# Grouped-query attention on one core: K transposed by the DMA engines instead of TensorE, with a new order of TensorE's work

## The chip, the cores and the metric

The kernel runs on one core of a Trainium2 chip. Times are device microseconds of one execution. A core has TensorE (PE, matmuls; PEld is its weight load), VectorE (DVE), ScalarE (ACT), GpSimd (POOL), SyncE (SP, which here only issues DMAs) and 16 DMA engines. Every "fast" run below is compared with fast runs of the kernel before on the same chip.

## The reference

Batch 8, sequence 512, 32 query heads, 8 KV heads, head dimension 64, all fp32. Four query heads share one KV head.

```python
scores  = einsum('bhqd,bhkd->bhqk', Q, K_expanded) / sqrt(64)
weights = exp(scores - max(scores))
weights = weights / (sum(weights) + 1e-10)
output  = einsum('bhqk,bhkd->bhqd', weights, V_expanded)
```

## The kernel before

Work is cut into 32 units (a batch and a pair of KV heads). A unit has 16 *score tiles* (128 keys x 2 heads x 512 queries). For each tile PE writes scores into one of three buffers in PSUM, the memory that its results go to. Then ACT (11 tiles of a unit) or DVE (5 tiles, with integer arithmetic that approximates the exponential) turns them into probabilities in SBUF, the core's working memory, and so frees the buffer. A unit also has 32 *output blocks*, each of four matmuls of probabilities with V, which fill one of two small output banks that DVE copies out.

Q and K come from HBM with the sequence on the partitions. Before they can be used in a score matmul they must be turned, so that the head dimension is on the partitions. PE does that with transposing matmuls (*turns*) into the same two output banks, and DVE copies the result out: 16 turns of Q and 4 of K per unit.

```python
def load_k(b):
    t = kn_pool.tile([128, SC, KV * D], BF16, name="k_nat")
    nc.gpsimd.dma_start(out=t, in_=rows(K, b, 0, KV))     # fp32 -> bf16, natural layout
    kn[b] = t
...
def mm_turn(f, at):                                       # one PE transpose, into an output bank
    ...
    nc.tensor.transpose(xs[f][:, at * 128:(at + 1) * 128], src, ident)

def take_turn(f):
    ...
    if part is None:                                      # K: DVE copy, then a swapped copy by DMA
        k = kt_pool.tile([128, 2, S], BF16, name="kt")
        nc.vector.tensor_copy(out=k[:, 0, :], in_=x[:, 0:S])
        nc.sync.dma_start(out=k[64:128, 1, :], in_=k[0:64, 0, :])
        nc.sync.dma_start(out=k[0:64, 1, :], in_=k[64:128, 0, :])
```

The program gives every engine its instructions in a fixed order. A small planner in Python sets that order when the kernel is built. Its inputs are lists per unit: `SCORES` says which of 16 tiles goes to ACT (A) or DVE (D), `FILL` how many output blocks or turns PE does behind each tile, `ORDER` the order of those (`o7` is seven output blocks that share a bank, `K4` four turns of K, `08` and `18` eight turns of Q).

```python
SCORES = "ADAAADAADAADAADA"
FILL = [0, 0, 8, 0, 0, 6, 9, 0, 0, 8, 0, 0, 12, 0, 0, 9]
ORDER = "K4 o6 o7 08 o7 18 o5 o7".split()
```

The softmax here doesn't subtract the row's maximum and nothing guards it: scores larger than these inputs give would overflow.

## Time and profile before

| | |
|---|---|
| time | 351.09 us, median of 3 (later 350.81, median of 12) |
| ACT, first to last exponential | 7.95 to 341.99 us of a span of 349.3 |
| ACT's period per unit, units 2 to 29 | 10.35 us |

The page of the kernel before: busy time of each engine, then the chain of work that ended last (by engine), then ACT's group of exponentials (busy us, mean ns of one; idle time before them and its releaser).

```profile
PE 337.0 (96%) x5774; PEld 224.6 (64%) x5774; DVE 329.3 (94%) x463; ACT 333.9 (96%) x356; POOL 280.3 (80%) x201
...
PE 48%; ACT 38%; POOL 4%; DVE 4%; issue 3%; DMA 1%; POOLq 0%; DVEq 0%; ACTq 0%
...
L288 ACT ACTIVATE pa<-s 128x1024 bf16<-128x1024 f32 x353 | 331.4, 1026 | 4.1 <-PE s L275 3.5
```

Four engines are busy for 80 to 96% of the span, so busy shares do not name the bottleneck. And ACT's idle time of 4.1 us is not all that it loses: the records (mean 1026 ns) overlap, so a small wait hides inside them. The Trainium skill, "Perfetto Trace Analysis", section "Summary: the profiler window per engine type", says that an ACT or DVE record runs from the start of the arithmetic to the acknowledged write, and leaves the rest out. This trace agrees with that picture: records of 1026 ns start 903 ns apart. The measure to use is therefore the distance from one start to the next.

The groups of PE and DVE that K's turns cost, as listed by form (columns as above):

```profile
L405 PE MATMUL x<-ident,k_nat 128*128 128x128 bf16 x124 | 17.3, 222 | 0.2 <-DMA k_nat<-in_K_dram 0.2
...
L412 DVE COPY kt<-x 128x512 bf16<-128x512 bf16 x31 | 11.3, 364 | 0.0
```

The chain of waits of the kernel before, which is the chain of work that ended last, from 150.9 us on (start, duration, what). It shows PE's order as the planner made it:

```profile
150.92 0.82 PE s L275 x6
151.74 0.97 PE x L334 x28
152.70 0.11 PE x L405 x2
152.82 0.85 PE s L275 x6
153.66 0.22 PE x L405 x2
153.88 0.72 PE x L334 x24
```

Between the score matmuls (`s`), PE does runs of output blocks (L334) and turns (L405) of very different length: 0.97 + 0.11 = 1.08 us, then 0.22 + 0.72 = 0.94 us.

### The profile page before, as it was taken

The numbers are of one execution on the slowest core, as the hardware profiler recorded it, in microseconds if no ns is written. First come the engines' busy times: TensorE is split into PE (matmuls) and PEld (weight loads), VectorE is DVE, ScalarE is ACT, GpSimd is POOL, SyncE is SP. The second block draws the span as 40 slices with busy tenths as digits, with TensorE's granted clock in tenths as the row PEclk, the third lists the DMA queues.
The fourth block names the chain that finished last, engine by engine and source line by source line (L and its number), as shares of the span: only waits on it lengthen the run. The fifth ranks groups of instructions, "written<-read, shape, count | busy, mean of one in ns | idle before, by whom it ended". The sixth has DMA issues, their size and how long they took to land.

```text
span 349.3 us, 12952 instructions
## 1 busy us (share of the span) xinstructions
PE 337.0 (96%) x5774; PEld 224.6 (64%) x5774; DVE 329.3 (94%) x463; ACT 333.9 (96%) x356; POOL 280.3 (80%) x201
## 2 busy tenths in 40 slices
PE   8799999999999999999999999999999999999992
PEld 3356666666676666666666666666666666666661
DVE  3899999999999999999999999999999999999982
ACT  3999999999999999999999999999999999999981
POOL 5279797879978798987979979787997879786693
PEclk9999999999999999999999999999999999999997
DMA  8989567898659958699886986789765996823338
GB/s 182 208 137 192 160 182 198 183 203 207 159 164 233 263 110 205 149 236 227 191 204 129 221 197 174 194 193 218 181 165 163 236 265 116 209 95 137 122 133 231
DMA packets 52007, 64.40 MB, mean 184 GB/s; under 512 B 3440, under 2 KB 36592, under 8 KB 51952
## 3 DMA queue, kind: packets, MB, share of 16 engines
q0 software_dynamic: 25344, 24.91, 47.3%
q1 hardware_dynamic: 25552, 38.28, 32.3%
q8 instruction: 45, 0.74, 0.8%
q10 hardware_dynamic: 1056, 0.39, 0.4%
q14 instruction: 10, 0.08, 0.1%
HBM read 50.86 MB, written 33.55 MB: 242 GB/s over the span
## 4 chain that ended last, share of the span: by engine, by line
PE 48%; ACT 38%; POOL 4%; DVE 4%; issue 3%; DMA 1%; POOLq 0%; DVEq 0%; ACTq 0%
ACT pa L288 38%; PE s L275 21%; PE x L334 19%; PE x L405 6%; POOL o_sb L378 2%; DMA kt<-kt 1%; DVE pd L305 1%; PE x L488 1%; POOL sum L321 1%; POOL hi L315 1%; DVE raw L357 1%; DVE qt L419 1%; PE x L500 0%; DVE lo L305 0%; DVE inv L373 0%
## 5 line engine op out<-in xcount | busy, mean ns | idle before, releaser
L288 ACT ACTIVATE pa<-s 128x1024 bf16<-128x1024 f32 x353 | 331.4, 1026 | 4.1 <-PE s L275 3.5
L275 PE MATMUL s<-qt,kt 64*128 64x512 bf16 x1024 | 163.2, 381 | 3.9 <-ACT pa L288 1.2
L305 DVE TENSOR_SCALAR pd<-s 128x1024 uint16<-128x1024 f32 x128 | 155.9, 1218 | 2.1 <-PE s L275 2.1
L334 PEld LDWEIGHTS <-pa 128*128 128x128 bf16 x2816 | 135.8, 97 | 29.2 <-issue 29.0
L334 PE MATMUL x<-v,pa 128*128 128x65 bf16 x2728 | 150.6, 194 | 0.2
L334 PE MATMUL x<-v,pd 128*128 128x65 bf16 x992 | 131.8, 194 | 0.2 <-DVE raw L357 0.2
L378 POOL TENSOR_TENSOR o_sb<-raw,inv 128x1024 f32<-128x1024 f32 (+1 forms) x64 | 118.8, 1880 | 1.7 <-DVE inv L373 1.3
L275 PEld LDWEIGHTS <-kt 64*128 64x128 bf16 x1024 | 55.8, 93 | 68.2 <-issue 37.4
L334 PEld LDWEIGHTS <-pd 128*128 128x128 bf16 x1024 | 98.8, 98 | 0.4 <-issue 0.2
L357 DVE COPY raw<-x 128x455 f32<-128x455 f32 (+3 forms) x159 | 91.8, 579 | 4.7 <-PE x L334 4.6
L315 POOL TENSOR_TENSOR hi<-lo,shift 128x512 int32<-128x512 int32 x32 | 40.6, 1270 | 48.6 <-PE x L334 39.3
L321 POOL TENSOR_TENSOR sum<-lo,hi 128x1024 bf16<-128x1024 bf16 x32 | 68.0, 2124 | 2.5
L405 PE MATMUL x<-ident,q_nat 128*128 128x128 bf16 x504 | 43.6, 220 | 0.1
L419 DVE COPY qt<-x 128x1024 bf16<-128x1024 bf16 x63 | 42.8, 680 | 0.0
L305 DVE TENSOR_SCALAR lo<-s 128x1024 uint16<-128x1024 f32 x32 | 39.1, 1221 | 0.5 <-PE s L275 0.5
L405 PEld LDWEIGHTS <-q_nat 128*128 128x128 bf16 x504 | 29.9, 98 | 7.9 <-issue 7.5
L334 PE MATMUL x<-v,sum 128*128 128x65 bf16 x248 | 34.7, 194 | 0.0
L245 POOL DMA_DIRECT2D q_nat<-in_Q_dram x32 | 25.5, 797 | 0.0
L334 PEld LDWEIGHTS <-sum 128*128 128x128 bf16 x256 | 25.0, 98 | 0.2 <-issue 0.2
L263 POOL COPY v<-v_nat 128x2048 bf16<-128x2048 bf16 x8 | 15.2, 1904 | 6.4 <-DMA v_nat<-in_V_dram 6.4
L405 PE MATMUL x<-ident,k_nat 128*128 128x128 bf16 x124 | 17.3, 222 | 0.2 <-DMA k_nat<-in_K_dram 0.2
L405 PEld LDWEIGHTS <-k_nat 128*128 128x128 bf16 x124 | 7.5, 98 | 7.4 <-issue 7.0
(35 smaller groups left out, 67.2 us busy)
## 6 DMA issues: line engine op xcount, KB each, us to landing
out_dram<-o_sb SPq DMA_DIRECT2D x30, 1024.0 KB, 5.2
q_nat<-in_Q_dram POOLq DMA_DIRECT2D x31, 512.0 KB, 6.0
k_nat<-in_K_dram POOLq DMA_DIRECT2D x8, 512.0 KB, 8.9
v_nat<-in_V_dram POOLq DMA_DIRECT2D x8, 512.0 KB, 10.6
kt<-kt SPq DMA_DIRECT2D x62, 64.0 KB, 5.1
out_dram<-o_sb SPq DMA_DIRECT2D x2, 512.0 KB, 3.6
out_dram<-o_sb SPq DMA_DIRECT2D x3, 256.0 KB, 3.9
q<-in_Q_dram ACTq DMA_DIRECT2D x1, 256.0 KB, 4.3
```

What stands on the lines that cost most here:

```text
L245: nc.gpsimd.dma_start(out=t[:, :, lo * D:], in_=rows(Q, b, HU * gp + lo, HU * (gp + 1)))
L263: nc.gpsimd.tensor_copy(out=t[:, :, :, 0:D], in_=vn.pop(b).rearrange("p sc (h d) -> p sc h d", h=KV))
L275: nc.tensor.matmul(s[:, m, :], kt[u][64 * m:64 * m + 64, 0 if m == g else 1, kc * 128:(kc + 1) * 128], qt[u][64 * m:64 * m + 64, i, :], st ...
L288: recent.append(nc.scalar.activation(out=pts[t][:, ms, :], in_=src[:, ms, :], func=mybir.ActivationFunctionType.Exp, scale=float(scale),))
L305: nc.vector.tensor_scalar(out=bits, in0=score.pop(t), scalar1=float(A_schr), scalar2=float(B_two if two else B_one), op0=mybir.AluOpType.mult,
L315: nc.gpsimd.tensor_tensor(out=high.rearrange("p m s -> p (m s)").bitcast(I32), in0=bits.rearrange("p m s -> p (m s)").bitcast(I32), in1=shift,
L321: nc.gpsimd.tensor_tensor(out=dst, in0=bits.bitcast(BF16), in1=high.bitcast(BF16), op=mybir.AluOpType.add)
L334: nc.tensor.matmul(xs[f][:, at * D1:(at + 1) * D1], pts[(u * HPG + i) * SC + kc][:, m, qc * 128:(qc + 1) * 128], v1[u][:, kc, 2 * i // HPG ...
L357: nc.vector.tensor_copy(out=raws[u][:, lo:lo + n, :], in_=x[:, 0:n * D1])
L378: eng.tensor_tensor(out=osbs[u].rearrange("p qc h d -> p h qc d")[:, lo // SC + h0:lo // SC + h0 + nh], in0=src[:, :, 0:D].rearrange("p (h ...
L405: nc.tensor.transpose(xs[f][:, at * 128:(at + 1) * 128], src, ident)
L419: nc.vector.tensor_copy(out=qt[u][:, 2 * part:2 * part + 2, :], in_=x)
```

## The change

Intent: take K's turns off PE and its copies off DVE for batches 1 to 7. K is cast to bf16 into a scratch tensor in HBM, and one DMA transpose per batch brings it turned into SBUF. The swapped copy is made by two DMAs per batch instead of eight. Units 0 to 3 still use PE. The freed time goes with a new order: a fill of seven output blocks behind each DVE tile. There are also more probability buffers, one output buffer fewer, an earlier start of the tiles that are summed (`EARLY`), and other lists for the first and the last two units (`HEAD`: 110 blocks and turns are done in the first two).

```diff
-    FILL = [0, 0, 8, 0, 0, 6, 9, 0, 0, 8, 0, 0, 12, 0, 0, 9]
-    ORDER = "K4 o6 o7 08 o7 18 o5 o7".split()
+    SCORES = "ADAADAADAADAAADA"
+    FILL = [0, 0, 7, 0, 0, 7, 0, 0, 7, 0, 0, 7, 0, 10, 0, 10]
+    ORDER = "o6 18 08 o7 o7 o7 o5".split()
+    EARLY = 3
+    HEAD = 110
 ...
     def load_k(b):
-        t = kn_pool.tile([128, SC, KV * D], BF16, name="k_nat")
-        nc.gpsimd.dma_start(out=t, in_=rows(K, b, 0, KV))
-        kn[b] = t
+        if b == 0:
+            ...
+            return
+        ks[b] = ks_pool.tile([S, KV * D], BF16, name="ks")                    # in HBM
+        nc.gpsimd.dma_start(out=ks[b], in_=K[b].rearrange("s h d -> s (h d)"))
+
+    def turn_k(b):
+        straight[b] = kt_pool.tile([128, GP, S], BF16, name="straight")
+        nc.sync.dma_start_transpose(out=straight[b], in_=ks.pop(b))
+
+    def swap_k(b):
+        t = straight.pop(b)
+        k = kt_pool.tile([128, GP, S], BF16, name="swapped")
+        nc.sync.dma_start(out=k[0:64], in_=t[64:128])
+        nc.sync.dma_start(out=k[64:128], in_=t[0:64])
 ...
-    pa_pool = ctx.enter_context(tc.tile_pool(name="pa", bufs=17))
+    pa_pool = ctx.enter_context(tc.tile_pool(name="pa", bufs=19))
 ...
-    osb_pool = ctx.enter_context(tc.tile_pool(name="osb", bufs=3))
+    osb_pool = ctx.enter_context(tc.tile_pool(name="osb", bufs=2))
 ... (order of the head and the tail, the planner's bookkeeping, names)
```

More of the change, by code (lines that the diff above doesn't have):

```diff
@@ L31, with __init__ @@
     DRAIN = 0.1
-    def __init__(self, nu, kind, order, groups, arrive, x_cost, x_behind, fix, nslot, nx, npt):
+    def __init__(self, nu, kind, early, head, order, groups, arrive, x_cost, x_behind, fix, nslot, nx, npt):
         self.ops = []
@@ L36, in __init__ @@
         qd = [t for t in range(16 * nu) if kind(t)]
-        pt, pair_done, parts = {}, {}, {(0, None): 0.0, (0, 0): 0.0}
+        rank = {t: i - (early + 0.5 if kind(t) == 2 else 0.0) for i, t in enumerate(qd)}
+        qd.sort(key=rank.get)
+        pt, pair_done = {}, {}
+        parts = {(u, None): 0.0 for u in [0, *range(4, nu)]}
+        parts[0, 0] = 0.0
         slots, xs = [0.0] * nslot, [0.0] * nx
@@ L42, in __init__ @@
         scoring = False
-        carry = 0
+        carry = done = 0
         behind = 0.0
@@ L66, in run_dve @@
                     if j[1] == "turn":
-                        swap = 0.0 if j[2][2] is not None else 3.0 if j[2][1] == 1 else 6.0
-                        parts[j[2][1:3]] = start + vis + swap
+                        parts[j[2][1:3]] = start + vis + (6.0 if j[2][2] is None else 0.0)
                     behind += x_behind(j[2])
@@ L83, in __init__ @@
             scores, fill = order(min(u, nu - 1))
+            carry = head - done if u == 2 else carry
             for k in range(16):
@@ L116, in __init__ @@
                 carry += fill[k]
-                loose = u < 1 or u >= nu - 2
-                while carry > 0 and gi < len(groups):
+                loose = u < 2 or u >= nu - 2
+                while carry > 0 and gi < len(groups) and (u > 1 or done < head):
                     f = groups[gi]
-                    if f[0] == "skip":
-                        step = min(carry, f[1] - at)
-                        carry, at = carry - step, at + step
-                        if at == f[1]:
-                            gi, at = gi + 1, 0
-                        continue
                     start = self.pe + (self.DRAIN if scoring else 0.0)
@@ L156, in __init__ @@
                     carry -= 1
+                    done += 1
                     if at == 0 and f[0] != "close":
@@ L168, in __init__ @@
                         gi, at = gi + 1, 0
-                carry = min(carry, 16)
+                carry = min(carry, 16 if u else 48)
         run_dve(NEVER)
@@ L196 @@
     NSLOT = 3
-    TILES = [int(c) for c in "0100010001020100"]
-    SCORES = "ADAAADAADAADAADA"
-    FILL = [0, 0, 8, 0, 0, 6, 9, 0, 0, 8, 0, 0, 12, 0, 0, 9]
-    ORDER = "K4 o6 o7 08 o7 18 o5 o7".split()
-    LAST_TILES = [int(c) for c in "0000200011010010"]
-    LAST = {
-        NU - 2: ("ADADAADAAAADADAA", [0, 0, 15, 32, 32, 0, 0, 0, 24, 0, 0, 0, 0, 0, 32, 3]),
-        NU - 1: ("DAADAADDAAAADAAA", [1, 32, 0, 7, 1, 0, 7, 0, 0, 0, 0, 1, 0, 20, 32, 9]),
+    TILES = [int(c) for c in "0100020100010001"]
+    SCORES = "ADAADAADAADAAADA"
[3 more added lines that the diff above has]
+    HEAD = 110
+    FIRST_TILES = [int(c) for c in "1010010200000010"]
+    LAST_TILES = [int(c) for c in "1200100001000100"]
+    SPECIAL = {
+        0: ("AADADAAAADAAADAD", [1, 28, 1, 0, 0, 2, 4, 15, 2, 8, 26, 0, 0, 2, 33, 0]),
+        1: ("AADAADADAADAAADA", [0, 1, 48, 0, 0, 0, 6, 0, 0, 7, 0, 4, 17, 0, 7, 8]),
+        NU - 2: ("ADAADAADAADAADAA", [0, 0, 7, 0, 0, 5, 2, 0, 8, 0, 0, 9, 0, 0, 21, 23]),
+        NU - 1: ("AADADADAADAAADAA", [5, 22, 0, 3, 0, 0, 2, 1, 2, 0, 0, 22, 24, 0, 0, 5]),
     }
-    SKIP = 22
     scale = 1.0 / math.sqrt(D)
@@ L217 @@
     qn_pool = ctx.enter_context(tc.tile_pool(name="qn", bufs=4))
-    kn_pool = ctx.enter_context(tc.tile_pool(name="kn", bufs=2))
+    ks_pool = ctx.enter_context(tc.tile_pool(name="ks", bufs=2, space=bass.MemoryType.DRAM))
     v_pool = ctx.enter_context(tc.tile_pool(name="v", bufs=1))
@@ L221 @@
     qt_pool = ctx.enter_context(tc.tile_pool(name="qt", bufs=4))
-    kt_pool = ctx.enter_context(tc.tile_pool(name="kt", bufs=4))
-    pa_pool = ctx.enter_context(tc.tile_pool(name="pa", bufs=17))
-    pd_pool = ctx.enter_context(tc.tile_pool(name="pd", bufs=7))
+    kt_pool = ctx.enter_context(tc.tile_pool(name="kt", bufs=2))
+    pa_pool = ctx.enter_context(tc.tile_pool(name="pa", bufs=19))
+    pd_pool = ctx.enter_context(tc.tile_pool(name="pd", bufs=8))
     lo_pool = ctx.enter_context(tc.tile_pool(name="lo", bufs=3))
     two_pool = ctx.enter_context(tc.tile_pool(name="two", bufs=2))
+    sum_pool = ctx.enter_context(tc.tile_pool(name="sum", bufs=3))
     raw_pool = ctx.enter_context(tc.tile_pool(name="raw", bufs=3))
-    osb_pool = ctx.enter_context(tc.tile_pool(name="osb", bufs=3))
+    osb_pool = ctx.enter_context(tc.tile_pool(name="osb", bufs=2))
     inv_pool = ctx.enter_context(tc.tile_pool(name="inv", bufs=4))
@@ L233 @@
     qn, kn, vn, v1 = {}, {}, {}, {}
+    ks, straight = {}, {}
     qt, kt = {}, {}
@@ L250, in load_k @@
     def load_k(b):
-        t = kn_pool.tile([128, SC, KV * D], BF16, name="k_nat")
-        nc.gpsimd.dma_start(out=t, in_=rows(K, b, 0, KV))
-        kn[b] = t
+        if b == 0:
+            kn[0] = first.tile([128, SC, KV * D], BF16, name="k_nat")
+            nc.gpsimd.dma_start(out=kn[0], in_=rows(K, b, 0, KV))
+            return
[9 more added lines that the diff above has]
+        nc.sync.dma_start(out=k[64:128], in_=t[0:64])
+        for gp in range(GP):
+            kt[GP * b + gp] = (t[:, gp, :], k[:, gp, :])
     def load_v(b):
@@ L276, in mm_scores @@
                 s[:, m, :],
-                kt[u][64 * m:64 * m + 64, 0 if m == g else 1, kc * 128:(kc + 1) * 128],
+                kt[u][int(m != g)][64 * m:64 * m + 64, kc * 128:(kc + 1) * 128],
                 qt[u][64 * m:64 * m + 64, i, :],
@@ L299, in exp_dve @@
         two = tile_kind(t) == 2
-        pts[t] = (two_pool if two else pd_pool).tile(
+        pts[t] = (sum_pool if two else pd_pool).tile(
             [128, 2, S], BF16, name="sum" if two else "pd"
@@ L351, in take_out @@
             divide(u, lo, n, nc.vector, x[:, 0:n * D1].rearrange("p (n c) -> p n c", c=D1))
-            if lo == 2 * BLK + 4:
-                store(u, 2 * BLK, BLK, nc.sync)
-            elif lo >= 3 * BLK:
-                store(u, lo, n, nc.scalar if lo == 3 * BLK else nc.sync)
+            if lo == 3 * BLK:
+                store(u, 2 * BLK, BLK, nc.scalar)
+                store(u, lo, n, nc.sync)
+            elif lo > 3 * BLK:
+                store(u, lo, n, nc.scalar)
             return
@@ L410, in take_turn @@
         if part is None:
-            k = kt_pool.tile([128, 2, S], BF16, name="kt")
+            k = first.tile([128, 2, S], BF16, name=f"kt{u}")
             nc.vector.tensor_copy(out=k[:, 0, :], in_=x[:, 0:S])
@@ L414, in take_turn @@
             nc.sync.dma_start(out=k[0:64, 1, :], in_=k[64:128, 0, :])
-            kt[u] = k
+            kt[u] = k[:, 0, :], k[:, 1, :]
         else:
@@ L424, in tile_kind @@
     def tile_kind(t):
-        return (LAST_TILES if t >= 16 * (NU - 1) else TILES)[t % 16]
+        return (FIRST_TILES if t < 16 else LAST_TILES if t >= 16 * (NU - 1) else TILES)[t % 16]
     turned = {}
-    groups = [("skip", 2), ("turn", 0, 1, 8), ("skip", 4), ("turn", 1, None, 4)]
-    groups += [("skip", SKIP - 6), ("turn", 1, 0, 8), ("turn", 1, 1, 8)]
+    groups = [("turn", 0, 1, 8), ("turn", 1, None, 4), ("turn", 1, 0, 8), ("turn", 2, None, 4)]
+    groups += [("turn", 1, 1, 8), ("turn", 3, None, 4)]
     for u in range(NU - 1):
@@ L455, in arrive @@
     def arrive(f):
-        return {(0, 1): 0.5, (1, None): 3.0}.get(f[1:3], 6.0 if f[1] == 1 else 0.0)
+        return {(0, 1): 1.0, (1, None): 3.6}.get(
+            f[1:3], 6.2 if f[1] == 1 else 11.4 if f[1] == 2 else 14.0 if f[1] == 3 else 0.0
+        ) if f[1:3] not in ((2, None), (3, None)) else 3.6
     plan = Plan(
-        NU, tile_kind, lambda u: LAST.get(u, (SCORES, FILL)), groups, arrive, x_cost, x_behind,
-        fix=6.0, nslot=NSLOT, nx=2, npt=6,
+        NU, tile_kind, EARLY, HEAD, lambda u: SPECIAL.get(u, (SCORES, FILL)), groups, arrive, x_cost, x_behind,
+        fix=6.0, nslot=NSLOT, nx=2, npt=7,
     )
@@ L493 @@
         nc.scalar.copy(out=q16[:, :, 0:2 * D], in_=q32[:, :, 0:2 * D])
-        kt[0] = kt_pool.tile([128, 2, S], BF16, name="kt")
+        k0 = first.tile([128, 2, S], BF16, name="kt0")
+        kt[0] = k0[:, 0, :], k0[:, 1, :]
         qt[0] = qt_pool.tile([128, HPG, S], BF16, name="qt")
@@ L501, in turn_first @@
             copy(out=dst, in_=x[:, 0:S])
-        turn_first(k16[:, :, 0, :], nc.vector.tensor_copy, kt[0][:, 0, :])
+        turn_first(k16[:, :, 0, :], nc.vector.tensor_copy, kt[0][0])
         turn_first(q16[:, :, 0:2 * D], nc.scalar.copy, qt[0][:, 0, :])
-        turn_first(k16[:, :, 1, :], nc.vector.tensor_copy, kt[0][:, 1, :])
+        turn_first(k16[:, :, 1, :], nc.vector.tensor_copy, kt[0][1])
         nc.vector.tensor_copy(out=q16[:, :, 2 * D:4 * D], in_=q32[:, :, 2 * D:4 * D])
@@ L512 @@
         load_q(3)
-        pending_first = True
+        scored = 0
+        spread_done = []
         due = False
@@ L524 @@
                 b, r = divmod(what[0], 16 * GP)
+                if what[0] == 4:
+                    load_k(1)
+                if r == 52 and b + 2 < B:
+                    load_k(b + 2)
+                if r == (8 if b else 20) and b + 1 < B:
+                    turn_k(b + 1)
                 if r == 24 and b + 1 < B:
-                    load_k(b + 1)
                     load_v(b + 1)
+                if r == (28 if b else 40) and b + 1 < B:
+                    swap_k(b + 1)
                 if r == 48 and b + 1 < B:
@@ L530 @@
                 mm_scores(*what)
-                if pending_first and what[0] > 0:
-                    pending_first = False
+                scored += 1
+                if scored == 1:
                     turn_first(q16[:, :, 2 * D:4 * D], nc.vector.tensor_copy, qt[0][:, 1, :])
-                    spread_v(0)
             elif engine == "act":
@@ L538 @@
                 exp_dve(what)
+                if 0 not in spread_done:
+                    spread_done.append(0)
+                    spread_v(0)
             if engine == "dve" and what_kind != "turn" and after and due:
```

## The prediction

> **What bounds it now.** The page has ACT busy 96%, PE 96%, DVE 94%: busy shares don't tell them apart, so I use the distances between starts in the timeline. Between 20 and 320 us a unit (16 score tiles: 11 exponentials on ACT, 5 on DVE) takes 10.34 us.
> - ACT: undisturbed exponentials start 903 or 920 ns apart; eleven make 10.02 us. The missing 0.32 us hides inside the records (mean 1026 ns): four or five exponentials a unit start 0.97 to 1.04 us after the one before.
> - DVE: undisturbed distances are 1.14 us (score tile), 0.55/0.47/0.40 (copies of 7/6/5 blocks), 0.60 (Q copy), 0.28 (K copy), 0.26 (reciprocal). A unit is 5x1.14 + 2.51 + 1.19 + 0.28 + 0.26 = 9.95 us, only 0.07 below ACT's floor.
> - PE: busy, but in the table of waits its weight loads wait on "issue" (37 us before scores); from its spacing I estimate 8.6 us of work.
>
> Two saturated engines interlock through three score buffers and two output banks. ACT's floor is highest, but DVE's lack of slack keeps it from it.
>
> **What changes.** For batches 1 to 7, K goes HBM fp32 -> HBM bf16 -> DMA transpose -> SBUF, with two half-swaps per batch instead of eight. Removed from 28 units: four PE transposes (estimate 0.23 us, PE's spacing) and one DVE copy (0.28 us effective; its record says 0.36). The 11:5 split is unchanged: ACT's work doesn't fall. DVE's floor becomes 9.67 us, 0.35 below ACT's. Also: fill is spread evenly, sum tiles start earlier, probability buffers are added, and the first two units do 110 fill blocks, leaving about 14 output blocks of backlog instead of 30.
>
> **Sum.**
> - Steady: the unit goes from 10.34 to about 10.08 us: 28 x 0.26 = 7.3 us.
> - Tail: ACT's last two units take 11.25 and 12.03 us, 3.2 us over the floor, catching up. 16 blocks fewer at about 0.12 us are 2 us; I count 1.5.
> - Head: ACT loses about 0.7 us around 18.6 us to unit 1's swapped K (a 5.0 us DMA in the chain of waits). Three K turns and one more load now stand there: 0.
>
> 351.1 - 8.8 = 342.3 us. With ACT always at its floor the gain would be about 13 us.
>
> **DMA.** Its share is 0.84 in the middle stretches. The Trainium skill, "DMA: Bandwidth & Descriptors", section "Latency and other measured facts", gives DMA transposes 261 GB/s; at that, 0.5 MB takes an estimated 2 us. No run yet shows it. The code leaves 20 score tiles (13 us) from transpose to swap and 36 (23 us) from swap to use, so one five times slower still hides. It stands in SP's queue ahead of output stores, which have two buffers now, not three: that is the danger.
>
> **Predicted: 342.3 us, 80% range 338.5 to 347.** Faster by over 2%: 0.66; within 2%: 0.31; slower: 0.03.
>
> **Right if** the timeline shows ACT at 10.05 to 10.15 us per unit, DVE with gaps before score tiles, K copies only for units 1 to 3, and the last two units' ACT waits halved. **Wrong if** the unit stays at 10.3 (the interlock sat in PE's order or the score buffers, not DVE); if the table of waits shows PE waiting on DMA for transposed or swapped K, or POOL waiting for output buffers behind SP's queue; or if K's extra HBM traffic delays loads in the first 30 us.

## More of the kernel before

For one unit (the 15th) the eleven distances between ACT's starts, in ns, are:

```
kernel before   920  904  903  903  941  920 1017  920 1009  920  968    sum 10325
```

903 ns is an exponential that did not wait. Three or four of the eleven start late.

DVE's waits for score tiles, from the table of who waited for whom (us in total, times, longest):

```profile
DVE pd L305 <- PE s L275: 2.1, 6, 0.7
```

## The result

| | kernel before | changed kernel |
|---|---|---|
| median, us | 350.81 (12 runs, 350.47 to 351.34) | 346.49 (10 runs, 345.75 to 347.79) |
| ratio | | 0.9876, 95% interval 0.9862 to 0.9891 |

A ratio is the mean time of one kernel's fast runs over that of the other's fast runs of the same rounds, so it is not quite the ratio of the medians. The gain is 4.3 us or 1.2%. It is inside the predicted range, near its slow end, and half of the 8.8 us that were forecast; "faster by over 2%", which had been given 0.66, did not happen.

The page of the changed kernel, the same parts as above:

```profile
PE 333.3 (97%) x5662; PEld 219.7 (64%) x5662; DVE 322.2 (94%) x435; ACT 329.6 (96%) x356; POOL 277.5 (81%) x201
...
PE 85%; ACT 10%; DVE 3%; issue 1%; DVEq 0%
...
L307 ACT ACTIVATE pa<-s 128x1024 bf16<-128x1024 f32 x353 | 327.2, 1023 | 4.6 <-PE s L294 4.3
```

DVE's busy time fell by 7 us and PE's by 4 us. ACT has the same 353 exponentials. The chain that ended last now runs 85% on PE, 48% before.

The chain of waits of the changed kernel, 123 to 131 us:

```profile
123.14 0.95 PE x L353 x28
124.09 0.89 PE s L294 x6
124.98 0.96 PE x L353 x28
125.94 0.90 PE s L294 x6
126.84 0.96 PE x L353 x28
127.80 0.89 PE s L294 x6
128.69 0.95 PE x L353 x28
129.64 0.54 PE s L294 x4
130.18 0.66 PE x L425 x10
```

The runs between the scores are now even: 0.95, 0.96, 0.96, 0.95 us (L353), then the turns of Q (0.66 us, L425). A score group of 0.89 or 0.90 us and a run of 0.96 us make 1.85 us, in which ACT does two exponentials; without waiting they would take 2 x 0.903 = 1.81 us. PE waits in this loop too: in the 111 groups of three score tiles in units 2 to 29 the second tile starts 0.227 us after the first (medians), but the third 0.335 us after the second, and in 109 of them 45 to 60 ns after an exponential has ended. So the third tile waits for the buffer that ACT frees, and the sum of PE's work is not what fills the 1.85 us.

The DMA issues of K's new path (what, engine, count, KB each where given, median us from issue to landing):

```profile
ks<-in_K_dram POOLq DMA_DIRECT2D x7, 512.0 KB, 9.2
swapped<-straight SPq DMA_DIRECT2D x14, 256.0 KB, 9.1
...
straight<-ks SPq DMA_TRANSPOSE x7, 9.5
```

From the starts of ACT's exponentials in the two profiles, the whole difference of the spans (349.3 and 344.1 us) can be placed. It is 5.2 us and not 4.3, because the profiled run of the changed kernel (345.86 us) is one of its fastest:

| part | before, us | changed, us | gain | predicted gain |
|---|---|---|---|---|
| start to first exponential | 7.95 | 7.61 | 0.3 | |
| first two units | 21.07 | 22.97 | -1.9 | 0 (head) |
| units 2 to 29 | 289.69 (10.346 each) | 285.82 (10.208 each) | 3.9 | 7.3 |
| last two units, to the last start | 23.28 | 21.42 | 1.9 | |
| last start to the end | 7.35 | 6.24 | 1.1 | 1.5 (both) |

The shortfall lies in the steady part: 3.9 us of 7.3. The head cost more and the tail gave more than said, and these two errors (1.6 and 1.5 us) all but cancel.

### The profile page after: what moved, and what is told of

The parts are those of the page before. It is cut to its first block, busy times and chain, and to the rows that moved or that the text cites. A ratio compares the mean times of both kernels' runs of the same rounds, so it can differ in the third digit from the quotient of the medians.

```text
span 344.1 us, 12637 instructions
## 1 busy us (share of the span) xinstructions
PE 333.3 (97%) x5662; PEld 219.7 (64%) x5662; DVE 322.2 (94%) x435; ACT 329.6 (96%) x356; POOL 277.5 (81%) x201
## 4 chain that ended last, share of the span: by engine, by line
PE 85%; ACT 10%; DVE 3%; issue 1%; DVEq 0%
PE s L294 39%; PE x L353 36%; ACT pa L307 10%; PE x L425 9%; PE x L510 1%; DVE pd L324 1%; DVE raw L377 1%; DVE lo L324 0%; DVE inv L393 0%; PE x L523 0%; DVE o_sb L398 0%; DVE kt L524 0%; DVE q L529 0%; DVE qt L524 0%; DVE warm L496 0%
## 5 line engine op out<-in xcount | busy, mean ns | idle before, releaser
L307 ACT ACTIVATE pa<-s 128x1024 bf16<-128x1024 f32 x353 | 327.2, 1023 | 4.6 <-PE s L294 4.3
L353 PEld LDWEIGHTS <-pa 128*128 128x128 bf16 x2816 | 130.7, 98 | 30.0 <-issue 29.2
L353 PE MATMUL x<-v,pa 128*128 128x65 bf16 x2728 | 144.1, 194 | 0.2 <-DVE o_sb L398 0.2
L294 PE MATMUL s<-qt,straight 64*128 64x512 bf16 x448 | 143.2, 382 | 0.8 <-ACT pa L307 0.7
L294 PE MATMUL s<-qt,swapped 64*128 64x512 bf16 x448 | 142.6, 380 | 0.4 <-ACT pa L307 0.2
L353 PE MATMUL x<-v,pd 128*128 128x65 bf16 x992 | 132.0, 194 | 0.1
L353 PEld LDWEIGHTS <-pd 128*128 128x128 bf16 x1024 | 98.3, 98 | 1.7 <-issue 1.4
L377 DVE COPY raw<-x 128x455 f32<-128x455 f32 (+3 forms) x159 | 88.8, 575 | 0.5 <-PE x L353 0.5
L294 PEld LDWEIGHTS <-straight 64*128 64x128 bf16 x448 | 32.4, 93 | 29.5 <-issue 24.6
L294 PEld LDWEIGHTS <-swapped 64*128 64x128 bf16 x448 | 34.0, 93 | 24.5 <-issue 12.8
L425 PEld LDWEIGHTS <-q_nat 128*128 128x128 bf16 x504 | 28.6, 98 | 18.2 <-issue 17.9
L425 PE MATMUL x<-ident,q_nat 128*128 128x128 bf16 x504 | 39.1, 220 | 0.0
L353 PE MATMUL x<-v,sum 128*128 128x65 bf16 x248 | 34.4, 193 | 0.0
L353 PEld LDWEIGHTS <-sum 128*128 128x128 bf16 x256 | 24.9, 97 | 0.0
L294 PE MATMUL s<-qt,kt 64*128 64x512 bf16 x128 | 21.4, 381 | 2.5 <-ACT pa L307 1.5
```

The lines of the kernel that those rows point to most:

```text
L294: nc.tensor.matmul(s[:, m, :], kt[u][int(m != g)][64 * m:64 * m + 64, kc * 128:(kc + 1) * 128], qt[u][64 * m:64 * m + 64, i, :], start=Tru ...
L307: recent.append(nc.scalar.activation(out=pts[t][:, ms, :], in_=src[:, ms, :], func=mybir.ActivationFunctionType.Exp, scale=float(scale),))
L353: nc.tensor.matmul(xs[f][:, at * D1:(at + 1) * D1], pts[(u * HPG + i) * SC + kc][:, m, qc * 128:(qc + 1) * 128], v1[u][:, kc, 2 * i // HPG ...
L377: nc.vector.tensor_copy(out=raws[u][:, lo:lo + n, :], in_=x[:, 0:n * D1])
```

## The experiments

Theory S is the prediction's: the K work taken off DVE (and PE) gives the steady gain, because DVE had no slack. Rival O: the gain comes from the new order. Theory L, formed from the chain of the changed kernel: the pace is set by PE's queue. ACT frees a score buffer, PE fills it, does the whole run of blocks that stands next in its order, and only then scores the tile that ACT needs next. What counts then is the length of each run behind a DVE tile, not the sum of PE's or DVE's work.

| run | what | time, us (before, same rounds) | ratio | unit, us, mean of units 2 to 29 |
|---|---|---|---|---|
| kernel before | | 350.81 | 1 | 10.346 |
| changed kernel | | 346.49 | 0.9876 | 10.208 |
| e1b_dma_only | K by DMA, old order | 352.85 (350.81) | 1.0043 | 10.398 (median 10.274) |
| e2b_plan_only | new order, K on PE and DVE | 360.13 (350.81) | 1.0266 | 10.697 (units 3 to 29) |
| e3b_dve_back | changed + DVE copy | 352.79 (350.81) | 1.0060 | 10.437 |
| e4_pe_back | changed + 4 turns on PE | 351.11 (350.95) | 1.0008 | 10.358 (median 10.324) |
| e5_short_out | changed, shorter runs on PE | 343.23 (350.81) | 0.9780 | 10.084 |
| e7b_before_no_recip | before, less DVE work | 350.79 (350.75) | 1.0001 | 10.346 |
| e8_two_turns | changed, DMA transposes twice | 346.59 (350.75) | 0.9878 | 10.220 (median 10.182) |
| e6_head_short | changed, shorter runs in the head | 349.19 (350.75) | 0.9947 | 10.265 (median 10.211) |
| e9_even_fill | changed, fill moved | 357.57 (350.75) | 1.0192 | 10.611 |
| e1_dma_only, e2_plan_only, e3_dve_back | void, see below | 393.39, 387.22, 408.18 (350.95) | 1.1208, 1.1031, 1.1607 | |

All profiles are of fast runs; one of the four runs of e1b_dma_only (356.81 us) was slow and is not in its ratio; the median of its three fast runs is 352.15 us, that of all four 352.85 us. The units are from one profile each. The distances between ACT's starts in the 15th unit, in ns, for the runs that the argument rests on:

```
kernel before          920  904  903  903  941  920 1017  920 1009  920  968    sum 10325
e7b_before_no_recip    920  905  904  904  937  920 1016  921 1009  921  967        10324
e1b_dma_only           903  904  903  903  967  920 1017  920 1009  920  903        10269
changed kernel         920  937  920  930  920  936  920  920  920  904  930        10157
e4_pe_back             921  975  921  904  907  973  921  904  919  904 1061        10310
e3b_dve_back           920 1109  920  903  903  981  920  903  920  904 1040        10423
e5_short_out           920  904  903  903  906  914  920  905  920  903  989        10087
```

### Three void runs, and what they say

The first three tries to undo or do one part alone went wrong by my edits, and each is worth a look.

> The kernel before, with its own fill order, buffers, head and tail, but K of batches 1 to 7 brought by the DMA transposes (28 K turns and K copies less). Theory S (the steady gain of 3.9 us comes from the work taken off the engines, DVE above all): ACT's unit falls from 10.34 to 10.2 us or lower and the time to about 347 us. Rival O (the gain comes from the new order of the fill): ACT's unit stays at 10.3 and the time at 350.5 us or above.

e1_dma_only took 393 us: I had taken the K blocks out of the fill of unit 2 although that unit still turns K, so from there on every run was two blocks out of step with the score tiles and the banks.

> The changed kernel with its order of the fill, its head and its tail, but every K turned by PE and copied by DVE, as before (the four K blocks stand ahead of the second run of transposes, the sums of the fill are 52 again). Theory S: the unit is back at 10.3 us, the time at 349.5 to 351 us (head and tail together gave 1.3 us). Rival O: the unit stays at 10.2 us and the time at about 347 us.

e2_plan_only took 387 us: the four K turns came right behind 16 turns of Q. The chain of waits shows turns (L421), then DVE's copy of one bank (`qt`, 0.69 us), a score tile on DVE, and the other copy, before PE may write on; ACT is not in the chain.

```profile
155.17 0.57 PE x L421 x8
...
155.76 0.69 DVE qt L436
156.46 0.56 DVE pd L320
...
157.50 0.69 DVE qt L436
```

> The changed kernel with one spare DVE copy per unit (a 128x256 copy of fp32 to bf16, about 0.28 us, that nobody reads) after a Q copy, for 28 units. Theory S: most of the steady gain is given back, 2 to 4 us more than the changed kernel's 346.5. If DVE's work did not matter (the gain sat in PE's transposes or in the order): less than 0.7 us more.

e3_dve_back took 408 us. The spare DVE copy, 28 times, took 1.9 us each. The same form took 0.29 us at the start of the same kernel. The timeline of DVE, and that of POOL at the same time (start, us, what):

```profile
164.35 1.93 DVE L441 CAST spare<-spare_in 128x256 bf16<-128x256 f32 x1
```

```profile
164.00 2.12 POOL L340 TENSOR_TENSOR sum<-lo,hi 128x1024 bf16<-128x1024 bf16 x1
```

The copy began while POOL ran a 2.12 us sum and ended when that did, at 166.1 to 166.3 us. All 28 copies did so: each began within a sum and ended about 0.15 us after it. That agrees with the Trainium skill, "SBUF — State Buffer", section "Who interferes with whom": a DVE cast from SBUF to SBUF can need the port pair that it shares with GpSimd, and the second to come is blocked for the whole instruction. My expectation ("about 0.28 us") was wrong by a factor of seven for that reason. A copy of the K copy's form out of the output bank took 0.41 us each time (e3b_dve_back).

The lesson of all three: the order and the work fit together closely. In e1_dma_only the engines had less work than before, and a slip of two blocks still made the unit 1.4 us longer (11.72 us), because each late step of one engine holds a buffer that another needs.

### e7b_before_no_recip: DVE's slack, given directly

```diff
-        nc.vector.reciprocal(out=inv, in_=src[:, :, D])
+        if 2 <= u < NU - 2:
+            inv = fixed[:, 0:n]          # a constant: wrong result on purpose
+        else:
+            nc.vector.reciprocal(out=inv, in_=src[:, :, D])
```

> Wrong result on purpose: the kernel before, without the reciprocal in units 2 to 29 (a constant in its place), so DVE has 0.26 us less in each, as much as the K copy took; PE, its order and ACT are untouched. The prediction's reading (DVE's lack of slack keeps ACT from its floor): the unit falls from 10.34 to 10.1 us, the time to 344 us. Theory L (what PE has to do behind a DVE tile sets ACT's gaps): the unit stays at 10.25 to 10.34 us, the time at 348.5 to 351.

Measured: ratio 1.0001 (0.9986 to 1.0016), unit 10.346 us, ACT's distances as before to within a few ns. The page and DVE's waits for score tiles:

```profile
PE 336.9 (97%) x5774; PEld 224.6 (64%) x5774; DVE 324.6 (93%) x435; ACT 333.7 (96%) x356; POOL 280.2 (80%) x202
```

```profile
DVE pd L305 <- PE s L275: 6.3, 31, 0.7
```

DVE did 4.7 us less work (324.6, 329.3 before) and waited longer and more often for scores (6.3 us, 31 times; 2.1 us, 6 times before). As much DVE time as a K copy took, given back, is worth nothing in the kernel before. (The reciprocal reads SBUF and holds no output bank, as a K copy does; what the bank is worth is left to the next run.) **That step of the prediction falls.**

### e1b_dma_only: K's work gone, old order

```diff
 (kernel before, with load_k, turn_k, swap_k and the K buffers of the changed kernel)
-            elif u + 2 < NU:
+            elif u + 2 < NU and (kind != "K" or u + 2 < 4):
-    FILL = [0, 0, 8, 0, 0, 6, 9, 0, 0, 8, 0, 0, 12, 0, 0, 9]
+    FILL = [0, 0, 6, 0, 0, 6, 9, 0, 0, 8, 0, 0, 12, 0, 0, 7]     # units 3 and later
```

The last two units' lists were set so that PE's order is that of the kernel before, block for block, without the K turns.

> The first try of this was void: its fill slipped by two blocks against the score tiles. Now PE's order is that of the kernel before, block for block, in all units, head and tail; only the K turns of units 4 to 31 are taken out and K comes by the DMA transposes. Theory S (the work taken off PE and DVE is what gives the steady gain): ACT's unit at 10.2 us or lower, time 346 to 348 us. Rival O (the new order gives it): the unit at 10.3 us, time 350 us or above.

Measured: 352.85 us (fast runs 352.15), ratio 1.0043, on the side of rival O and not of theory S. The median unit is 10.274 us, 0.07 us less than before (28 x 0.07 = 2.0 us), so the work that was removed is worth about a quarter of what the prediction gave it. In the profiled run two stalls in units 4 and 20 (counted from 0), together 3.3 us, ate more than that; PE's weight loads stand there for 2.0 and 1.6 us in a wait that the profile books as "issue", that is, waiting for nothing that it shows.

ACT's distances say why. Of the three latest starts of the kernel before, only the last one (968 ns) is gone; it stood behind a run that ended with two K turns. Those of 1017 and 1009 ns are unchanged: their runs had no K in them. And one start became later (941 to 967 ns), which gave part of the gain back. The chain of waits of e1b_dma_only:

```profile
150.61 0.50 PE x L425 x7
151.11 0.61 PE x L354 x20
151.72 0.82 PE s L295 x6
152.54 0.97 PE x L354 x28
```

The run of 0.50 + 0.61 = 1.11 us (seven turns of Q, five output blocks) is still there, next to a run of 0.97 us.

### e2b_plan_only: the new order, with K on PE and DVE

```diff
 (changed kernel, with K's loads, turns and copies as before for all units)
-    ORDER = "o6 18 08 o7 o7 o7 o5".split()
+    ORDER = "o6 18 08 o7 K4 o7 o7 o5".split()
-    FILL = [0, 0, 7, 0, 0, 7, 0, 0, 7, 0, 0, 7, 0, 10, 0, 10]
+    FILL = [0, 0, 7, 0, 0, 9, 0, 0, 8, 0, 0, 8, 0, 10, 0, 10]    # units 3 and later
```

> The first try was void: three transposing groups in a row had to share two banks. Now the changed kernel's order with the four K blocks per unit between two output groups (fill 7, 9, 8, 8 behind the DVE tiles in place of 7, 7, 7, 7), turned by PE and copied by DVE. Theory S: unit about 10.3 to 10.4 us, time 349 to 353 us. Rival O: unit 10.2 us, time about 347 us.

Measured: 360.13 us, unit 10.697 us, slower than either theory said. In each of units 3 to 29 one exponential starts 1.22 to 1.30 us after the one before, and in most of them two more start 1.0 to 1.13 us after. So the new order alone, with K put back in this place, is worse than the old one. I do not claim that no order with K on PE reaches 10.2 us; this one does not.

### e3b_dve_back and e4_pe_back: each engine's share put back

```diff
 e3b_dve_back, in take_turn, behind the copy of Q:
+            if u >= 4 and part == 1:
+                nc.vector.tensor_copy(out=spare, in_=x[:, 0:S])
 e4_pe_back, in mm_turn, ahead of the turns of Q (overwritten by them):
+            for x4 in range(4 if u >= 4 and part == 1 else 0):
+                nc.tensor.transpose(xs[f][:, x4 * 128:(x4 + 1) * 128], qn[u][:, x4, 256:384], ident)
```

> The first try's spare copy took 1.9 us instead of 0.28 us, so it said nothing about 0.28 us. Now the spare DVE copy reads 128x512 bf16 from the output bank, as the K copy did (0.36 us in the record, 0.28 us effective), after a Q copy, for 28 units. If DVE's time sets the pace: 3 to 6 us more than the changed kernel's 346.5. If DVE has the slack that the changed trace shows (gaps of about 0.09 us after each copy of a full group, 0.3 us a unit) and PE sets the pace: under 2 us more.

> The changed kernel with four spare transposes per unit on PE, written to a bank that the real transposes overwrite, for 28 units. Theory S, with DVE as what gave the gain and PE with slack: under 1 us more than 346.5. Theory L (after the change the pace is set by the loop of PE's queue, the three score buffers and ACT, so PE's time counts): 3 to 6 us more, that is 0.1 to 0.2 us a unit.

Measured: e3b_dve_back 352.79 us, 6.3 us over the changed kernel, unit 10.437 us. e4_pe_back 351.11 us, 4.6 us over it, unit 10.358 us, which is no better than the kernel before. Either share alone, put back in one place, takes the whole gain away. For e3b_dve_back the chain of waits names DVE beside PE:

```profile
DVE 36%; PE 36%; ACT 18%; DMA 4%; issue 4%; POOL 0%; SPq 0%; DVEq 0%; ACTq 0%
```

(The spare copy also holds its bank 0.3 us longer, so part of its cost may be that.) The expectation that DVE has slack to spare (under 2 us) failed. In the changed kernel PE and DVE are both in the ring: time added to either, in the place tried, shows up at ACT.

### e5_short_out: shorter runs

```diff
+        short = 2 <= u < NU - 2
         kcs = {"open": range(SC - 1), "close": range(SC - 1, SC)}.get(
-            step, range(SC))
+            step, range(SC - 1 if short else SC))                  # wrong result on purpose
```

> Wrong result on purpose: the changed kernel with three instead of four matmuls in each output block of units 2 to 29, which takes about 0.24 us of PE's time from behind every DVE tile; ACT and DVE keep their work. Theory L (what keeps ACT from its floor after the change is PE's queue: ACT frees a score buffer, PE fills it, does the output blocks, and only then scores the next tile): ACT's unit falls from 10.21 to its floor, 10.0 to 10.05 us, time 340.5 to 342 us. If DVE or ACT itself sets the pace: the unit stays at 10.2 us, the time at 346 us.

Measured: 343.23 us, unit 10.084 us. The page of e5_short_out, busy times and the chain by engine:

```profile
PE 313.8 (92%) x4766; PEld 192.7 (57%) x4766; DVE 321.2 (94%) x435; ACT 326.3 (96%) x356; POOL 277.7 (82%) x201
...
ACT 84%; DMA 6%; PE 5%; POOL 2%; issue 1%; DVE 1%; SPq 0%; DVEq 0%
```

DVE's and ACT's work is the same, PE has a quarter less of output work, and the chain that ended last moves from PE (85%) to ACT (84%). Nearly all of ACT's distances are now 903 to 920 ns. So PE's runs are what kept ACT from 10.08 us in the changed kernel. The expectation of 340.5 to 342 us was 1 to 3 us too low, since one start per unit stays late (989 ns). This run also corrects ACT's floor: distances of 903 and 904 ns stand in a row here, so eleven make 9.94 us, not the 10.02 us that the prediction took. By that floor the shorter runs brought back 0.12 of the 0.27 us that the changed kernel loses in each unit. The 920 ns that the prediction called undisturbed come, in the kernel before, mostly right behind a late start (106 of 117).

### e8_two_turns: the DMA path doubled

```diff
+        again = first.tile([128, GP, S], BF16, name="again")
+        nc.sync.dma_start_transpose(out=again, in_=ks[b])
         nc.sync.dma_start_transpose(out=straight[b], in_=ks.pop(b))
```

> The changed kernel with every DMA transpose done twice (the first into a tile that nobody reads), so K's part of the DMA work on SP's queue is more than doubled. If the DMA path is off the critical path: within 0.7 us of 346.5. If DMA time is what ate half of the expected gain: 2 us more or worse, with PE waiting on the swapped K or POOL on the output buffers.

Measured: 346.59 us, ratio 0.9878 (changed kernel 0.9876). Its DMA issues:

```profile
again<-ks SPq DMA_TRANSPOSE x7, 10.7
straight<-ks SPq DMA_TRANSPOSE x7, 8.4
```

With 14 transposes instead of 7 in SP's queue the time does not change. PE waits for the swapped K in one place only, at 46 to 47 us (0.9 us before a weight load and 0.4 us before a matmul in the table of waits), where the first K that came by DMA is used; unit 3 takes 10.99 us there. In the changed kernel it never does. Apart from that place the DMA path is off the critical path even when doubled.

### e6_head_short: the head

```diff
+        short = u == 0 or (u == 1 and lo < 13)                     # wrong result on purpose
```

(with three matmuls per block there, as in e5_short_out)

> Wrong result on purpose: the changed kernel with three instead of four matmuls in the output blocks that PE does during the first two units (unit 0 and the start of unit 1), 1.4 us less PE time there. If the head's loss (ACT's first two units take 22.97 us, 21.07 in the kernel before) is output work moved forward from the tail: those two units fall to 21.5 to 22.2 us, the time to 345 to 345.8. If it is the added K load or the K turns (DMA, DVE): they stay at 22.9 us, the time at 346.5.

Measured: 349.19 us (347.71 to 349.50), and ACT's first two units take 23.11 us, not less than the 22.97 us of the changed kernel. By the expectation's rule that would speak for the K load or the K turns and against the output work, but the time rose as well, and the chains show that this run cannot decide it. In the changed kernel's chain the head runs on PE, with 16 turns and then 56 matmuls of output between score tiles:

```profile
18.84 1.00 PE x L425 x16
19.84 0.79 PE s L294 x6
...
20.64 1.86 PE x L353 x56
```

With PE's share cut, the chain of e6_head_short runs on DVE instead, one K or Q copy, score tile and bank copy after the other:

```profile
16.94 0.33 DVE kt L435
17.27 1.13 DVE pd L324
18.41 0.47 DVE raw L380
18.88 1.13 DVE lo L324
```

So both engines are full in the head, and cutting one is not enough. Whether the K turns of units 2 and 3, which were moved here, or the output work is to blame for the 1.9 us was not separated. In the profiled run (347.71 us) the time is lost in two stalls in units 18 and 26 (11.35 and 11.00 us instead of 10.2), like those of e1b_dma_only.

### e9_even_fill: a try to beat both

```diff
-    FILL = [0, 0, 7, 0, 0, 7, 0, 0, 7, 0, 0, 7, 0, 10, 0, 10]
+    FILL = [0, 0, 7, 0, 0, 6, 0, 0, 7, 0, 0, 6, 0, 12, 0, 10]
```

> A try to beat both, correct result: the changed kernel with the fill 7, 6, 7, 6, 12, 10 in place of 7, 7, 7, 7, 10, 10, so that two output blocks stand ahead of the ten transposes, where PE has time left. Theory L: two of the four gaps of 0.93 to 0.94 us a unit go to 0.903 or 0.92, the unit falls by 0.03 to 0.06 us, the time by 1 to 1.6 us to about 345. If banks or DVE get in the way: the unit grows by 0.05 us or more.

Measured: 357.57 us, unit 10.611 us; correct, and 3% slower than the changed kernel. The chain of waits:

```profile
154.03 0.56 PE s L294 x4
154.58 0.36 PE x L353 x8
...
155.03 0.58 DVE raw L377
...
155.65 0.27 PE x L425 x2
```

Two output blocks (8 matmuls) right ahead of the turns finish their bank too late: the turns (L425) must wait until DVE has copied it out (0.58 us). In the changed kernel the last output bank of a unit ends a score group earlier. An even run length is not enough; here the bank had also to be closed a score group before it was needed again. No version tried here beats the changed kernel with a correct result.

## Why the prediction was right or wrong

- **Time.** 346.49 us lies in the stated 338.5 to 347, but the gain was 4.3 us and not 8.8, and the class given 0.66 was the wrong one. That the time is inside the range is no credit to the mechanism: the range was wide enough to hold half the gain, and the errors in head and tail happened to cancel.
- **The step that failed: "DVE's lack of slack keeps it from it", and with it "the unit goes from 10.34 to about 10.08 us: 28 x 0.26 = 7.3 us".** The unit went to 10.21 us, 3.9 us in all, which is neither the prediction's "right" (10.05 to 10.15) nor its "wrong" (10.3). e7b_before_no_recip gave DVE 0.26 us of slack in the kernel before and gained nothing. e1b_dma_only removed K's work and gained 0.07 us in its median unit. DVE's work per unit was close to the period, but it did not set it.
- **What stands in its place.** ACT starts late behind PE's long runs. In the kernel before this is read from the trace, not tested: between 127 and 133 us three exponentials start 1033, 1012 and 965 ns after the one before, and the score tiles that they read come behind runs of 1.01 us (seven output blocks, one turn of Q), 1.11 us (seven turns of Q, five blocks) and 1.07 us (seven blocks, two turns of K). Only the last of the three had K in it, and only that late start went away when K did (e1b_dma_only). That late starts follow PE holds over all of units 2 to 29: 95 of the 106 starts that come more than 930 ns after the one before lie 30 to 60 ns behind the end of a score matmul, and only 17 of the 202 others. In the changed kernel it is tested: shorter runs bring the unit to 10.08 us (e5_short_out), a longer one to 10.36 us (e4_pe_back). DVE time is not free there either (e3b_dve_back, 10.44 us), but with DVE's work unchanged e5_short_out reached 10.08 us, so it was not DVE that held the unit at 10.21. The gain came with K out of the two banks *and* even runs together; neither half gained as much alone in the orders tried (e1b_dma_only, e2b_plan_only). The added probability buffers and the earlier sum tiles were not tested alone. The prediction did name this as a way to be wrong ("the interlock sat in PE's order or the score buffers"), but gave it no number. Its check "DVE with gaps before score tiles" came true: in units 2 to 29 DVE stands idle in front of score tiles for 0.22 us a unit, under 0.01 us before the change. But the check cannot tell the theories apart: e7b_before_no_recip has 0.15 us there, and gained nothing.
- **PE's "8.6 us of work"** was a sum over a unit. With a fixed order and three score buffers the sum says little here; the length of each run does.
- **Tail: right in kind, undersized.** Predicted 1.5 us, measured 1.9 us in the last two units and 1.1 us behind the last exponential.
- **Head: wrong.** Predicted 0, measured a loss of 1.9 us in the first two units and 0.3 us gained before them. In the profile both engines are full there; the cause was not separated.
- **DMA: right.** K copies by DVE remain only for the first units, the transposes hide (e8_two_turns: the same time with twice as many), and neither the third output buffer nor SP's queue was missed: POOL waited once for an output buffer, 0.7 us. The estimate of 2 us per transpose was far off (9.5 us from issue to landing), but the 13 us left for it were enough.
- **Left open.** The changed kernel spreads more from run to run (2.0 us, the kernel before 0.9 us), and three profiles with K by DMA (e1b_dma_only, e6_head_short, e4_pe_back) show one or two stalls of 0.4 to 1.9 us in which PE waits for nothing that the page names. (The stall of e8_two_turns is the wait for the swapped K above.) The traces hold a lead that no run followed up. DMA queue q8 moves packets of 16 KB: 37, 44 and 45 of them in runs with 9,532, 11,324 and 11,548 matmuls and weight loads on PE, so one for about 256. The page calls it an instruction queue, so these are, by that count, PE's own instructions. The four stalls of e1b_dma_only and e6_head_short each end 1.2 to 1.6 us after such a packet has landed, and these four packets started later than any other in all the traces: PE had by then begun 388 to 445 instructions more than 256 for each earlier packet, and never more than 377 elsewhere. That points to PE running out of instructions. It is argued from four cases and not tested, and why the packets were late is open.

## What to carry to other kernels

When all engines are 90% busy, measure the distance between the starts of the costliest one and look, for each late start, at what the engine that it waits for did just before: here it was the length of that one run, and which buffer it holds, that counted, not an engine's total. Before crediting a change with "slack" on an engine, give that engine slack in the old kernel with a deliberately wrong result; here that one run (e7b_before_no_recip) showed 0 us where the forecast counted on 7.3. Moving work to the DMA engines paid here only together with a new order; taken alone it made the unit 0.07 us shorter.

## What the Trainium skill lacked or had wrong

- "DMA: Bandwidth & Descriptors", "Latency and other measured facts", gives 261 GB/s for DMA transposes with a non-contiguous middle dimension, and more for contiguous ones. A transpose of 512x512 bf16 from HBM into SBUF, next to other traffic, took 9.5 us from issue to landing: 524,288 bytes / 9.5 us = 55 GB/s. Issuing it kept SP busy for 3.5 to 5.7 us; the page has no time for issuing a transpose of this size.
- "TensorE: Matmul & The Clock Gate", "Part 4: PE-mode transpose", gives about 275 ns for a 128x128 transpose inside a kernel. Here the record is 220 ns, but in the chain of the changed kernel ten in a row take 0.66 us, about 66 ns each. The page has no back-to-back figure for transposes.
- "Perfetto Trace Analysis", "Identifying the Most-Contended Engine", takes ACT's and DVE's occupancy as a measure and LDWEIGHTS busy time for PE. For ACT that agrees: its occupancy was 96%, and its floor of 9.94 us is 96% of the unit of 10.35 us. For PE it misled: the weight loads were at 64% in the changed kernel, while the chain that ended last ran 85% on PE and shorter runs on PE made the unit 0.12 us shorter (e5_short_out). No page describes a pace set by the order of an in-order queue and a few PSUM buffers.
- "SBUF — State Buffer", "Who interferes with whom", was right and was overlooked: a 0.29 us DVE cast from SBUF to SBUF took 1.9 us beside POOL.
